# Sums of reciprocals on one core: where VectorE's sums write what nobody reads, in which row order, and how many products VectorE makes

## The chip, the cores and the metric

The kernel runs on one core of a Trainium2 chip. A core has TensorE (PE), VectorE (DVE), ScalarE (ACT), GpSimd (POOL) and SyncE (SP), each with its own instruction stream; they meet through semaphores. Sixteen DMA engines move data between the chip's main memory (HBM) and the on-chip memories. The metric is the device time of one execution in microseconds (us), lower is better.

## The reference

```python
def reference(x: np.ndarray) -> np.ndarray:
    return np.sum(1.0 / x, axis=-1).astype(np.float32)
```

`x` is 32 x 512 x 1024 float32, the absolute value of normal random numbers plus 1e-6. The result has 32 x 512 sums, each over 1024 reciprocals. That is 67.1 MB to read and 64 KB to write.

## The kernel before

The 16,384 rows are spread over 128 partitions, 128 rows on each. "Row" below means one such row index, that is, 128 rows of 1024 numbers at once, one on each partition (512 KB).

The kernel uses 1/a + 1/b = (a + b) / (a b). A row is cut into two halves of 512 numbers, a and b. For each row somebody makes the product a b, ScalarE takes its reciprocal as exp(-ln(S a b)) with S = 2^17, and VectorE multiplies this with something and adds everything up to one number per partition (the sum instruction of line 92, with the scale S and an accumulated output, followed by a tiny instruction that writes the accumulator into column c of the tile `sums`). That sum instruction also has an ordinary output, of as many elements as it has inputs, that nobody reads afterwards.

The work is cut into chunks of m = 2 rows, each a triple (m, e, v):

- A = (2, 0, 0): e = 0. GpSimd makes the products of both rows (line 136). ScalarE writes the reciprocals into a PSUM tile `rc` (line 151). VectorE sums each row whole: 1024 numbers of the row, times the reciprocal, which is read twice.
- B = (2, 2, 0): e = 2. GpSimd makes both products. TensorE adds a + b into PSUM tiles `s` by multiplying with the identity matrix (line 82, two matmuls for a row in the program, four in the profile). ScalarE writes the reciprocals back into the product tile `pr` (line 157). VectorE sums 512 numbers, `pr` times `s`.
- C = (2, 2, 1): like B, but with v = 1 the first row's product is VectorE's (line 125), from the row's first half and a copy of the second half that TensorE put into a PSUM tile `b`; GpSimd makes the product of the other row only.

`LOADS` lists the DMAs, all issued by SyncE in order: ten loads of four chunks (8 rows, 4 MB, rows 0 to 79), eight of two chunks (2 MB), eight of one (1 MB). They go into `ring`, 40 rows long, so a load waits until every reader and writer of the rows 40 earlier has finished. Of a load's chunks, the VectorE products come first in program order; then, chunk by chunk, GpSimd's products, TensorE's adds, the sums of the chunk before (`waiting`), and this chunk's ScalarE work. `keep` fixes each engine's order to the program's. So VectorE's sums always run one chunk behind.

Waits come from the tiles: whoever writes over data waits for those who read it or wrote it before, engine by engine. An instruction carries one wait; further ones become separate wait instructions in front of it. The sums of an A chunk write their useless output over the ring row they read (`out=row`); those of B and C write it over the product row they read. The product tiles `pr` come from one pool of six tiles, 4 KB on each partition; the tiles `s` from three PSUM buffers, `rc` from two, `b` from one. The last four loads are one chunk each: A, B, A, C.

Of the kernel before, what the change touches and what calls it, by code (L numbers as in the profile page):

```python
# [1 line left out]

# [6 lines left out]


@with_exitstack
def kernel(
    ctx: ExitStack,
    tc: tile.TileContext,
    x: bass.AP,
    out: bass.AP,
):

    nc = tc.nc
    f32 = mybir.dt.float32
    P = 128  # L30
    D = 1024
    H = D // 2
    F = 128

    R = 40

    S = float(2**17)

    A, B, C = (2, 0, 0), (2, 2, 0), (2, 2, 1)
    LOADS = [[A, B, A, C]] * 10 + [[A, B], [A, C]] * 4 + [[A], [B], [A], [C]] * 2

    Ln = mybir.ActivationFunctionType.Ln
    Exp = mybir.ActivationFunctionType.Exp
    mult = mybir.AluOpType.mult
    plus = mybir.AluOpType.add

    x_v = x.flatten_outer_dims().rearrange("(p f) d -> p f d", p=P)
    out_v = out.flatten().rearrange("(p f) -> p f", p=P)  # L50

    act_sets = list(get_activation_tables(nc.m.arch).keys())
    nc.scalar.add_instruction(  # L53
        mybir.InstLoadActFuncSet(
            name=nc.get_next_instruction_name(),
            act_func_set_id=act_sets.index("natural_log_exp_and_others"),
            ins=[],
            outs=[],
        )
    )  # L60

    ppool = ctx.enter_context(tc.tile_pool(name="ppool", bufs=6))
    opool = ctx.enter_context(tc.tile_pool(name="opool", bufs=1))
    spool = ctx.enter_context(
        tc.tile_pool(name="spool", bufs=3, space=bass.MemoryType.PSUM)
    )
    bpool = ctx.enter_context(
        tc.tile_pool(name="bpool", bufs=1, space=bass.MemoryType.PSUM)
    )
    rpool = ctx.enter_context(  # L70
        tc.tile_pool(name="rpool", bufs=2, space=bass.MemoryType.PSUM)
    )

    ring = opool.tile([P, R, D], f32)
    sums = opool.tile([P, F], f32)
    ident = opool.tile([P, P], f32)
    make_identity(nc, ident)
    keep = tc.keep_in_program_order

    def add(bank, *halves):  # L80
        for k, half in enumerate(halves):
            i = nc.tensor.matmul(  # L82
                bank,
                lhsT=ident,
                rhs=half,
                start=k == 0,
                stop=k == len(halves) - 1,
            )
            keep(i)

    def sum_row(c, row, fac):
        i = nc.vector.tensor_tensor_reduce(  # L92
            out=row,
            in0=row,
            in1=fac,
            scale=S,
            scalar=0.0,
            op0=mult,
            op1=plus,
            accum_out=sums[:, c : c + 1],  # L100
        )
        keep(i)

    def sum_rows(c, xc, pr, sm, rc):
        m, e = xc.shape[1], len(sm)
        for j in range(e, m):
            row = xc[:, j, :].rearrange("p (h e) -> p h e", h=2)
            sum_row(c + j, row, rc[:, j - e, :].unsqueeze(1).to_broadcast([P, 2, H]))
        for j in range(e):
            sum_row(c + j, pr[:, j, :], sm[j])  # L110

    waiting = None
    c0 = 0
    for chunks in LOADS:
        n = sum(m for m, _, _ in chunks)
        xt = ring[:, c0 % R : c0 % R + n, :]
        keep(nc.sync.dma_start(out=xt, in_=x_v[:, c0 : c0 + n, :]))

        made, q = [], 0
        for m, e, v in chunks:  # L120
            pr = ppool.tile([P, m, H], f32, tag="pr")
            for j in range(v):
                b = bpool.tile([P, H], f32, tag="b")
                add(b, xt[:, q + j, H:])
                i = nc.vector.tensor_tensor(  # L125
                    out=pr[:, j, :], in0=xt[:, q + j, :H], in1=b, op=mult
                )
                keep(i)
            made.append(pr)
            q += m  # L130

        q = 0
        for (m, e, v), pr in zip(chunks, made):
            xc = xt[:, q : q + m, :]
            if v < m:
                i = nc.gpsimd.tensor_tensor(  # L136
                    out=pr[:, v:, :], in0=xc[:, v:, :H], in1=xc[:, v:, H:], op=mult
                )
                keep(i)
            sm = []  # L140
            for j in range(e):
                s = spool.tile([P, H], f32, tag="s")
                add(s, xc[:, j, :H], xc[:, j, H:])
                sm.append(s)
            if waiting:
                sum_rows(*waiting)
            keep(nc.scalar.activation(out=pr, in_=pr, func=Ln, scale=S))  # L147
            rc = None
            if e < m:
                rc = rpool.tile([P, m - e, H], f32, tag="rc")  # L150
                i = nc.scalar.activation(  # L151
                    out=rc, in_=pr[:, e:, :], func=Exp, scale=-1.0
                )
                keep(i)
            if e:
                r = pr[:, :e, :]
                keep(nc.scalar.activation(out=r, in_=r, func=Exp, scale=-1.0))  # L157
            waiting = c0 + q, xc, pr, sm, rc
            q += m
        c0 += n  # L160
    assert c0 == F, c0
    sum_rows(*waiting)

    nc.sync.dma_start(out=out_v, in_=sums)


# [1 line left out]
_INS = ['x']  # L168
_OUTS = [((32, 512), 'float32')]


# [23 lines left out]
```

## Time and profile before

| | |
|---|---|
| median of 7 runs | 172.31 us (172.21 to 172.39) |
| the profiled execution's own time | 172.31 us |
| its span, from the first instruction to the last | 170.5 us |
| PE busy | 135.2 us, 79% |
| DVE busy | 124.6 us, 73% |
| ACT busy | 133.5 us, 78% |
| POOL busy | 133.0 us, 78% |
| granted TensorE clock | 0.998 |
| HBM read | 67.11 MB, 394 GB/s over the span |

Busy time counts arithmetic instructions, not waits, branches or the issuing of DMAs; busy PE includes pipelined matmuls whose ends are modelled. L92 is line 92 of the kernel. A row of a timeline gives start, duration, engine, line, operation, output <- input, shape, and in brackets the idle time before it with what ended it. The chain that ended last is followed back from the last instruction: at each step to what released it, or to the instruction before it on its engine. A stretch's row gives, for each engine, the busy time and the number of instructions, then the granted clock, the mean busy share of the sixteen DMA engines and their rate in GB/s.

### The profile page before, as it was taken

The numbers are of one execution on the slowest core, as the hardware profiler recorded it, in microseconds if no ns is written. First come the engines' busy times: TensorE is split into PE (matmuls) and PEld (weight loads), VectorE is DVE, ScalarE is ACT, GpSimd is POOL, SyncE is SP. The second block draws the span as 40 slices with busy tenths as digits, with TensorE's granted clock in tenths as the row PEclk, the third lists the DMA queues.
The fourth block names the chain that finished last, engine by engine and source line by source line (L and its number), as shares of the span: only waits on it lengthen the run. The fifth ranks groups of instructions, "written<-read, shape, count | busy, mean of one in ns | idle before, by whom it ended". The sixth has DMA issues, their size and how long they took to land.

```text
span 170.5 us, 1320 instructions
## 1 busy us (share of the span) xinstructions
PE 135.2 (79%) x288; PEld 51.9 (30%) x288; DVE 124.6 (73%) x272; ACT 133.5 (78%) x129; POOL 133.0 (78%) x70
## 2 busy tenths in 40 slices
PE   0008999888889888796988887979999998896790
PEld 0003333332332333242333322333334332342240
DVE  0001777777987777787777769889998988889683
ACT  3002979979787997959799797899999988999790
POOL 1008969696996969589696969999999799996930
PEclk9999999999999999999999999999999999999999
DMA  5999999999999999999999999999999999999300
GB/s 208 415 454 407 454 423 446 415 461 415 448 407 446 415 454 419 438 425 430 430 438 423 438 396 427 427 427 430 427 427 423 427 413 423 421 421 417 148 0 15
DMA packets 3895, 67.25 MB, mean 394 GB/s; under 512 B 432, under 2 KB 560, under 8 KB 560
## 3 DMA queue, kind: packets, MB, share of 16 engines
q1 hardware_dynamic: 3888, 67.18, 92.4%
q8 instruction: 2, 0.03, 0.1%
q14 instruction: 5, 0.04, 0.1%
HBM read 67.11 MB, written 0.07 MB: 394 GB/s over the span
## 4 chain that ended last, share of the span: by engine, by line
DMA 66%; POOL 22%; issue 6%; DVE 3%; ACT 1%; DVEq 0%; POOLq 0%
DMA ring<-in_x_dram 66%; POOL pr L136 22%; DVE ring L92 2%; ACT pr L147 1%; ACT rc L151 1%; DVE pr L92 0%; DVE pr L125 0%; DVEq L190 0%; POOLq L136 0%; DVE sums L92 0%; DVEq L92 0%
## 5 line engine op out<-in xcount | busy, mean ns | idle before, releaser
L136 POOL TENSOR_TENSOR pr<-ring 128x1024 f32<-128x1024 f32 x64 | 132.3, 2097 | 29.9 <-DMA ring<-in_x_dram 29.6
L82 PE MATMUL s<-ring,ident 128*128 128x512 f32 x256 | 120.1, 605 | 15.5 <-DVE sums L92 13.9
L92 DVE CUSTOM_DVE_ANT_1 ring<-ring,rc 128x1024 f32<-128x1024 f32 x64 | 75.6, 1219 | 26.9 <-ACT rc L151 22.8
L147 ACT ACTIVATE pr<-pr 128x1024 f32<-128x1024 f32 x64 | 67.3, 1051 | 30.0 <-POOL pr L136 29.6
L82 PEld LDWEIGHTS s<-ring,ident 128*128 128x128 f32 x256 | 46.6, 191 | 87.1 <-issue 47.9
L92 DVE CUSTOM_DVE_ANT_0 pr<-pr,s 128x512 f32<-128x512 f32 x64 | 41.3, 682 | 0.7 <-ACT pr L157 0.7
L157 ACT ACTIVATE pr<-pr 128x1024 f32<-128x1024 f32 x32 | 33.8, 1058 | 1.0
L151 ACT ACTIVATE rc<-pr 128x1024 f32<-128x1024 f32 x32 | 32.9, 1028 | 1.0
L82 PE MATMUL b<-ring,ident 128*128 128x512 f32 x32 | 18.6, 665 | 15.9 <-DMA ring<-in_x_dram 15.7
L125 DVE TENSOR_TENSOR pr<-ring,b 128x512 f32<-128x512 f32 x16 | 10.9, 683 | 15.7 <-PE b L82 15.6
L82 PEld LDWEIGHTS b<-ring,ident 128*128 128x128 f32 x32 | 5.2, 196 | 26.9 <-issue 15.0
L92 DVE DVE_READ_ACCUMULATOR2_ANT sums<- 128x1 f32 x128 | 10.6, 83 | 0.0
L53 ACT ACT_TABLE_LOAD x1 | 1.3, 1283 | 0.7 <-PEq L179 0.7
masks.py:197 POOL MEMSET ident<- 128x128 f32 x1 | 0.2, 204 | 0.3 <-POOLq L179 0.3
masks.py:199 POOL TENSOR_SCALAR_AFFINE_SELECT ident<-ident 128x128 f32<-128x128 f32 x1 | 0.3, 292 | 0.1
L179 POOL MEMSET const-float32-0.0<- 128x1 f32 x1 | 0.1, 98 | 0.2 <-issue 0.2
L179 POOL MEMSET const-uint8-127<- 128x1 uint8 x1 | 0.1, 103 | 0.0
L179 POOL MEMSET const-bfloat16-1.0<- 128x1 bf16 x1 | 0.1, 101 | 0.0
L179 POOL MEMSET const-float32-1.0<- 128x1 f32 x1 | 0.1, 98 | 0.0
## 6 DMA issues: line engine op xcount, KB each, us to landing
ring<-in_x_dram SPq DMA_DIRECT2D x10, 4096.0 KB, 37.6
ring<-in_x_dram SPq DMA_DIRECT2D x8, 2048.0 KB, 36.9
ring<-in_x_dram SPq DMA_DIRECT2D x8, 1024.0 KB, 28.4
out_dram<-sums SPq DMA_DIRECT2D x1, 64.0 KB, 1.5
```

The source lines that it names most:

```text
L53: nc.scalar.add_instruction(mybir.InstLoadActFuncSet(name=nc.get_next_instruction_name(), act_func_set_id=act_sets.index("natural_log_exp_ ...
L82: i = nc.tensor.matmul(bank, lhsT=ident, rhs=half, start=k == 0, stop=k == len(halves) - 1,)
L92: i = nc.vector.tensor_tensor_reduce(out=row, in0=row, in1=fac, scale=S, scalar=0.0, op0=mult, op1=plus, accum_out=sums[:, c : c + 1],)
L125: i = nc.vector.tensor_tensor(out=pr[:, j, :], in0=xt[:, q + j, :H], in1=b, op=mult)
L136: i = nc.gpsimd.tensor_tensor(out=pr[:, v:, :], in0=xc[:, v:, :H], in1=xc[:, v:, H:], op=mult)
L147: keep(nc.scalar.activation(out=pr, in_=pr, func=Ln, scale=S))
L151: i = nc.scalar.activation(out=rc, in_=pr[:, e:, :], func=Exp, scale=-1.0)
L157: keep(nc.scalar.activation(out=r, in_=r, func=Exp, scale=-1.0))
L179: nc = _bacc.Bacc("TRN2", target_bir_lowering=False, num_devices=1)
```

## The change

Four edits. In the first 80 rows, the loads alternate between A, B, A, B and A, B, A, C, so VectorE makes one product in 16 rows there, not one in 8 (five fewer in all; GpSimd makes those five). The sum of the first row of an A chunk writes its unread output over the chunk's own product tile, which ScalarE has read by then, and not over the ring; the second row's still goes over its ring row. The sums of a B or C chunk go through their rows in reverse. The product tiles come from two sets of four, one for A chunks (`pr`) and one for B and C chunks (`ps`), instead of one set of six.

```diff
-    LOADS = [[A, B, A, C]] * 10 + [[A, B], [A, C]] * 4 + [[A], [B], [A], [C]] * 2
+    LOADS = [[A, B, A, B], [A, B, A, C]] * 5 + [[A, B], [A, C]] * 4 + [[A], [B], [A], [C]] * 2
...
-    ppool = ctx.enter_context(tc.tile_pool(name="ppool", bufs=6))
+    ppool = ctx.enter_context(tc.tile_pool(name="ppool", bufs=4))
...
-    def sum_row(c, row, fac):
+    def sum_row(c, row, fac, out=None):
         i = nc.vector.tensor_tensor_reduce(
-            out=row,
+            out=row if out is None else out,
             in0=row,
...
         for j in range(e, m):
             row = xc[:, j, :].rearrange("p (h e) -> p h e", h=2)
-            sum_row(c + j, row, rc[:, j - e, :].unsqueeze(1).to_broadcast([P, 2, H]))
-        for j in range(e):
+            sum_row(
+                c + j,
+                row,
+                rc[:, j - e, :].unsqueeze(1).to_broadcast([P, 2, H]),
+                pr[:, e : e + 2, :] if j == e and m - e > 1 else None,
+            )
+        for j in reversed(range(e)):
             sum_row(c + j, pr[:, j, :], sm[j])
...
-            pr = ppool.tile([P, m, H], f32, tag="pr")
+            pr = ppool.tile([P, m, H], f32, tag="ps" if e else "pr")
```

## The prediction

> **What bounds the kernel now.** I read the page's slices first, then its chain, then the chain's last 40 us in order of time.
>
> ```profile
> DMA  5999999999999999999999999999999999999300
> DMA packets 3895, 67.25 MB, mean 394 GB/s; under 512 B 432, under 2 KB 560, under 8 KB 560
> q8 instruction: 2, 0.03, 0.1%
> q14 instruction: 5, 0.04, 0.1%
> DMA 66%; POOL 22%; issue 6%; DVE 3%; ACT 1%; DVEq 0%; POOLq 0%
> ```
>
> The DMA row is 9 from slice 2 to slice 36: the input stream never pauses. No arithmetic engine is that full. The two "instruction" rows are small packets in which the chip loads program code; they come back below.
>
> The stream's pace is read from POOL, which takes each 4 MB load as it lands (timeline, POOL):
>
> ```profile
> 62.40 8.28 POOL L136 TENSOR_TENSOR pr<-ring 128x1024 f32<-128x1024 f32 x4 [1.46 <-DMA ring<-in_x_dram]
> 72.96 8.25 POOL L136 TENSOR_TENSOR pr<-ring 128x1024 f32<-128x1024 f32 x4 [2.29 <-DMA ring<-in_x_dram]
> 82.68 8.25 POOL L136 TENSOR_TENSOR pr<-ring 128x1024 f32<-128x1024 f32 x4 [1.47 <-DMA ring<-in_x_dram]
> 92.39 8.27 POOL L136 TENSOR_TENSOR pr<-ring 128x1024 f32<-128x1024 f32 x4 [1.46 <-DMA ring<-in_x_dram]
> ```
>
> A load comes every 9.72 us, POOL needs 8.27 and idles 1.46. One interval is 10.56: something delayed a load by 0.84 us. Loads are issued 37.6 us (median of the page's DMA issues) before they land, so four are queued at once, and a ring slot could come free some 27 us later (37.6 less one load) before the stream noticed.
>
> The tail, by the chain in order of time and DVE's timeline:
>
> ```profile
> 131.49 25.59 DMA ring<-in_x_dram
> 157.24 2.36 POOL pr L136
> 159.71 2.38 POOL pr L136
> 162.11 1.07 ACT pr L147
> 163.20 1.04 ACT rc L151
> 164.23 0.03 DVEq L92
> 164.35 0.60 DVE ring L92
> ```
>
> ```profile
> 161.81 0.69 DVE L92 CUSTOM_DVE_ANT_0 pr<-pr,s 128x512 f32<-128x512 f32 x1 [0.66 <-ACT pr L157]
> ...
> 166.64 0.68 DVE L92 CUSTOM_DVE_ANT_0 pr<-pr,s 128x512 f32<-128x512 f32 x1
> ```
>
> So the end is the landing at 157.08 of the last B load plus two POOL products, ACT, and four sums on DVE. Who makes that landing late? Each load ends with sixteen small writes, one per DMA engine (the 432 packets under 512 B are 27 transfers times 16). Their times in the trace's packets show thirteen engines finishing the last load by 159.62 us and three late ones, at 160.49, 160.72 and 161.56. The stretches of the stream's end show the same:
>
> ```profile
> 159.60:160.40 0.80, 0.80 (x3) 0.21 (x2) 0.80 (x3) 0.77 (x1) 0.69 (x1) 1.00 0.17 72
> 160.50:160.70 0.20, 0.20 (x1) 0.00 (x0) 0.20 (x1) 0.19 (x1) 0.20 (x1) 1.00 0.10 41
> 160.75:161.50 0.75, 0.13 (x1) 0.00 (x0) 0.39 (x2) 0.75 (x1) 0.75 (x1) 1.00 0.05 22
> ```
>
> The last two columns are DMA share and GB/s; one engine of sixteen is 0.0625. Three engines, then two, then a single one are still at work.
>
> Why are those three late? Following each engine's end from load to load (9.70 us apart), single engines step back for good, each right behind a code packet: 8 KB at 46.25 us steps one by 0.97 us; 16 KB at 64.73 another by 1.56; 8 KB at 105.5 to 105.9 two, one of them the engine of 46.25 again, by 0.97; 16 KB at 131.37 a fifth by 1.54; 8 KB at 154.08 the engine of 46.25 a third time, by about 0.96. That last step is why the landings of the end, 2.48 apart till 153.75, jump to 157.08. Its engine had 0.14 us less delay than the slowest until then; it ends 0.84 later than the next (161.56 against 160.72). A load counts as landed 0.45 us after the slowest engine's write.
>
> Whose code? By the trace's records (waits counted), DVE had started 69, 199 to 201 and 325 instructions at 46.25, 105.5 to 105.9 and 154.08: steps of about 128, on the same DMA engine each time. ACT stands at 67 at the 8 KB of 73.04 and POOL at 68 at that of 105.5. PE stands at 195 and 449 at the two 16 KB packets, 254 apart. So a queue fetches when it has passed about 64, 192 and 320 instructions (PE: 192, 448, next 704).
>
> **The change part by part.** The profiled execution took 172.31 us for a span of 170.5; the median is 172.31, so its sums stand for the median.
>
> *Five fewer products on VectorE.* Gone: 5 DVE products of 0.683, 10 identity matmuls of 0.665 with their weight loads. Five POOL products grow from 1.279 to 2.370 us, 5.5 us in all, one per second 4 MB load. POOL's starts lie 2.33 apart, so such a load takes 3 x 2.33 + 2.37 = 9.36 us against 9.72 between landings: it still fits, with 0.36 idle. If that cover went, the next load has 1.46 idle, and the ring's 27 us lie behind. From row 80 the loads are unchanged, and POOL waits for landings again at 136.5, 141.5, 153.9 and 157.2. Cost: nothing.
>
> *First sum of an A chunk writes the product tile.* 32 of the 64 1.219 us sums keep their size. No row shows this sum with another destination; from below and above the nearest rows are the sums that write that tile over 512 elements (0.682) and the ring write (1.219); I take 1.219, same elements and reads. All but the last lie beside the stream. The wait for POOL moves to the second sum, which starts 1.15 later, long after it is met. In the tail, the first sum started 0.12 us behind ACT's end (164.23 to 164.35, over a separate wait); the B sum at 161.81, whose ACT wait is in the sum itself, 0.03 behind. Gain 0.09 in that hand-over.
>
> *Two pools of 4 instead of one of 6.* POOL's products for A now wait for DVE's sum of eight chunks earlier, about 19 us, where DVE trails by some 7 (product at 92.39, sums over at 99.35). Nothing waits: nothing.
>
> *Reverse rows.* The last chunk C sums row 1 first, so it needs the second of PE's sums first. That semaphore rose at 166.63, 4.62 us behind the last landing (162.01); the first's at 164.91. Now DVE started C at 166.64, so the old order hid it and the new one cannot. Elsewhere PE is some 3 us ahead of DVE: nothing.
>
> *Instructions.* Built, the programs hold on DVE 364 before and 322 after (5 products and 37 separate waits fewer), POOL 123 and 132, ACT 178 and 173, SP 73 and 74. PE loses about 14 of 589 records. DVE's last sum is then behind instruction 316, so its third fetch, due near 320, falls behind the input stream or never. The others keep their number: POOL's and ACT's second would be due near 192, PE's third near 704, and SP passes 64 only in the closing.
>
> *The sum.* Without that step the slowest engine ends at 160.72 instead of 161.56: landings -0.84 from the last B load on; the last one at 161.17. POOL follows (it was free at 156.25, the B load lands at 156.23). DVE would be free for C at 166.64 - 0.84 - 0.09 = 165.71, but PE's second sum comes at 161.17 + 4.62 = 165.79, and 0.12 for the hand-over gives 165.91. Before it was 166.64: -0.73. Two sums, the store and the closing follow as before. 172.31 - 0.73 = **171.58 us**.
>
> Bounds: the hand-over between 0.03 and 0.12 (I take 0.12, the row with a separate wait, as C will have); the step between 0.84 and 1.07, if the engine ending at 160.72 is relieved too (its PE fetch moves by some 16 instructions). That gives 171.26 to 171.58.
>
> A rule that speaks against this: the Trainium skill, "Runtime: NRT & Kernel Launch", section "Instruction fetch mechanics", has code streamed in 16 KiB blocks by the sequencer's own DMA queue, the cost mostly hidden. Hidden it is from DVE here, which works through 154.08 without a gap (153.71 to 154.37, then the next); the DMA engine's delay of 0.96 us is in the trace all the same, and DVE's packets are 8 KB. By the rule the sum would have no -0.84 and would be 172.42.
>
> **The rivals.**
>
> *The stream ends as before.* For it: the link from code packet to engine is by timing and counts, and the packet could be another queue's or come at another count. Then only the reversed tail counts: C at 166.63 + 0.12 = 166.75, +0.11: 172.42.
>
> *Slower: a code packet hits the engine that serves DVE.* PE's two came on two engines, DVE's on one, so the choice isn't explained. If PE's second went to DVE's, that would end at 160.60 + 1.54 = 162.14, landing at 162.59, 0.58 later than now: C at 167.21 + 0.12 against 166.64, 173.0. It decides as soon as any engine ends behind 161.56. Against it: DVE's engine was the same three times.
>
> *POOL as the bound.* It would need more than 9.72 / 4 = 2.43 us per product, and then over two loads 19.4 us against 9.36 + 8.27; the products measure 2.37 throughout. That loses almost nothing even so.
>
> *More gained.* If PE's packets left the late engines too, the stream would end with the thirteen (159.62). Then POOL would be the limit: free at 153.32 from the product before, it would start the tail's next one at 153.4 instead of 153.88 and the last B's 1.4 earlier; DVE would reach C at 166.64 - 1.44 - 0.09 = 165.1: 170.8.
>
> **How the numbers follow.** Forecast 0.78, stream as before 0.11, slower 0.07 (POOL in it), more gained 0.04. A difference under 0.2% (0.34 us) is about what this kernel's times cannot tell from none. The forecast and "more" are faster: 0.82; the second is within 0.2%: 0.11; slower 0.07. The range runs from 171.2, the lower bound of the forecast, to 172.45, the stream as before.
>
> **What would show it.** Right: one code packet less before the stream's end, none near 154; landings 2.48 apart to the last, at about 161.2; C's first sum waiting on PE. Product loads of about 9.36 on POOL with 0.36 idle. Wrong: a jump of 0.8 in the landings behind row 120, or a fourth late engine.

## The result and the profile after

The changed kernel takes 171.77 us (median of 13 runs, 171.59 to 171.95) against 172.34 us of the kernel before on the same chips (31 runs). The ratio is 0.9967, 95% interval 0.996 to 0.9975: 0.57 us, or 0.33%, faster. The forecast was 171.58, with a range of 171.2 to 172.45; the measured time is in that range, and 0.19 above the sum and its own bounds (171.26 to 171.58). The profiled execution took 171.90 us for a span of 170.1, so it lies 0.13 above the median.

The page after, in the lines that answer to those of before (span, the DMA row of the slices, code packets, chain):

```profile
span 170.1 us, 1267 instructions
DMA  6999999999999999999999999999999999999400
q8 instruction: 2, 0.03, 0.1%
q14 instruction: 5, 0.03, 0.0%
DMA 80%; POOL 7%; issue 3%; PE 3%; ACT 3%; DVE 2%; SPq 1%; POOLq 0%; DVEq 0%
```

The stream is as full as before. What the code rows say is small but it is the point: queue 14 moved 0.03 MB, not 0.04 (its count stays at 5, because a packet of 24 bytes at 0.16 us is counted in it). One 8 KB packet of VectorE's has left the span: by the packets' times it now comes at 170.76, behind the last instruction of the span. In the end of the stream, 150 to 161 us, no code packet is left at all (DMA view of that stretch, all its queues):

```profile
## 3 DMA queue, kind: packets, MB, share of 16 engines
q1 hardware_dynamic: 537, 3.85, 84.1%
```

Before, the same view had a row "q14 instruction: 1" for the packet of 154.08. POOL and TensorE show what came of it (timelines after; the last row is TensorE's first work on the last load):

```profile
73.11 9.31 POOL L141 TENSOR_TENSOR pr<-ring 128x1024 f32<-128x1024 f32 x4 [2.42 <-DMA ring<-in_x_dram]
82.83 8.28 POOL L141 TENSOR_TENSOR pr<-ring 128x1024 f32<-128x1024 f32 x4 [0.41 <-DMA ring<-in_x_dram]
92.54 9.35 POOL L141 TENSOR_TENSOR pr<-ring 128x1024 f32<-128x1024 f32 x4 [1.43 <-DMA ring<-in_x_dram]
153.96 8.73 POOL L141 TENSOR_TENSOR pr<-ring 128x1024 f32<-128x1024 f32 x4 [0.58 <-DMA ring<-in_x_dram]
```

```profile
161.30 1.13 PE L82 MATMUL b<-ring,ident 128*128 128x512 f32 x2 [1.17 <-DMA ring<-in_x_dram]
```

The loads with four whole products take POOL 9.31 to 9.35 us and leave 0.41 before the next one: the fit that was worked out. From 153.96 on POOL works without a break; before, it had to wait at 157.24 for a late landing. The last load lands at 161.25 instead of 162.01.

The stretches of the stream's end after, in the same columns as before, lose the single engine that was still at work till 161.56:

```profile
159.60:160.60 1.00, 0.52 (x2) 0.00 (x0) 1.00 (x3) 0.97 (x2) 1.00 (x1) 1.00 0.18 74
160.90:161.25 0.35, 0.00 (x0) 0.00 (x0) 0.30 (x3) 0.13 (x1) 0.35 (x1) 1.00 0.00 0
```

Three engines (0.18 is three of sixteen) end almost together now, at 160.65, 160.70 and 160.83 by their small writes; the other thirteen are through by 159.53. The chain of the tail has a new last link (chain in order of time, then one row of the waits):

```profile
141.49 19.76 DMA ring<-in_x_dram
161.30 1.13 PE b L82 x2
162.42 3.45 PE s L82 x8
165.90 0.05 DVEq L92
166.04 0.69 DVE pr L92
```

```profile
DVE pr L92 <- PE s L82: 0.2, 1, 0.2
```

Before, the chain ran over POOL and ACT to VectorE. Now it runs from the last landing straight over TensorE, and the last chunk's first sum is the only one in the kernel that waits for TensorE's sums, for 0.17 us.

### The profile page after: what moved, and what is told of

Its sections match the earlier page's. It is cut to its first block, busy times and chain, and to the rows that moved or that the text cites. A ratio compares the mean times of both kernels' runs of the same rounds, so it can differ in the third digit from the quotient of the medians.

```text
span 170.1 us, 1267 instructions
## 1 busy us (share of the span) xinstructions
PE 133.3 (78%) x278; PEld 51.3 (30%) x278; DVE 122.4 (72%) x267; ACT 133.9 (79%) x129; POOL 138.3 (81%) x70
## 4 chain that ended last, share of the span: by engine, by line
DMA 80%; POOL 7%; issue 3%; PE 3%; ACT 3%; DVE 2%; SPq 1%; POOLq 0%; DVEq 0%
DMA ring<-in_x_dram 80%; POOL pr L141 7%; PE s L82 2%; ACT pr L152 2%; DVE ring L92 1%; DVE pr L92 1%; SPq L122 1%; PE b L82 1%; ACT rc L156 1%; ACT pr L162 0%; DVE sums L92 0%; POOLq L141 0%; DVEq L92 0%; DVEq L195 0%
## 5 line engine op out<-in xcount | busy, mean ns | idle before, releaser
L141 POOL TENSOR_TENSOR pr<-ring 128x1024 f32<-128x1024 f32 x64 | 137.6, 2181 | 23.8 <-DMA ring<-in_x_dram 22.4
L82 PE MATMUL s<-ring,ident 128*128 128x512 f32 x256 | 124.0, 624 | 31.1 <-DMA ring<-in_x_dram 15.5
L82 PEld LDWEIGHTS s<-ring,ident 128*128 128x128 f32 x256 | 47.4, 195 | 104.4 <-issue 63.6
L92 DVE CUSTOM_DVE_ANT_1 pr<-ring,rc 128x1024 f32<-128x1024 f32 x32 | 39.1, 1221 | 43.9 <-ACT rc L156 43.9
L92 DVE CUSTOM_DVE_ANT_1 ring<-ring,rc 128x1024 f32<-128x1024 f32 x32 | 38.9, 1216 | 0.0
L82 PE MATMUL b<-ring,ident 128*128 128x512 f32 x22 | 12.0, 629 | 1.4 <-DMA ring<-in_x_dram 1.4
L130 DVE TENSOR_TENSOR pr<-ring,b 128x512 f32<-128x512 f32 x11 | 7.5, 684 | 0.8 <-PE b L82 0.7
L82 PEld LDWEIGHTS b<-ring,ident 128*128 128x128 f32 x22 | 4.0, 202 | 9.3 <-DMA ring<-in_x_dram 7.1
```

Source lines behind the costliest of these rows:

```text
L82: i = nc.tensor.matmul(bank, lhsT=ident, rhs=half, start=k == 0, stop=k == len(halves) - 1,)
L92: i = nc.vector.tensor_tensor_reduce(out=row if out is None else out, in0=row, in1=fac, scale=S, scalar=0.0, op0=mult, op1=plus, accum_out ...
L130: i = nc.vector.tensor_tensor(out=pr[:, j, :], in0=xt[:, q + j, :H], in1=b, op=mult)
L141: i = nc.gpsimd.tensor_tensor(out=pr[:, v:, :], in0=xc[:, v:, :H], in1=xc[:, v:, H:], op=mult)
```

## The experiments

The theory: the gain is one code packet of VectorE's that no longer comes while the input streams. Its rivals: VectorE's lighter work, the moved waits or the row order brought the gain. All kernels were timed beside the kernel before on the same chip; the chips differ in noise, so each time is to be held against its own "before".

### One part alone: the reversed rows

```diff
-        for j in range(e):
+        for j in reversed(range(e)):
             sum_row(c + j, pr[:, j, :], sm[j])
```

> The kernel before with one edit: the sums of a B or C chunk go through their rows in reverse. Its VectorE program holds 357 instructions (before 364). Theory (the gain is a code packet that no longer comes while the input streams): VectorE still passes instruction 320 some 33 instructions before its end, so the third packet comes at about 156 us, the slowest DMA engine still ends near 161.56, and the reversed tail adds what it added after the change, a hand-over of 0.12 to 0.17 us behind TensorE's second sum: 172.4 to 172.5. Rival (the row order itself brought the gain): 171.8.

Measured: 172.84 us, before 172.52; ratio 1.0021, 0.9995 to 1.0046. No gain, so the rival is out; the loss is larger than expected but not clear of none. POOL's timeline shows the packet delaying the load after the one that it delayed in the kernel before, where it came at 154.08 and POOL waited at 157.24 (here it came at 156.11, with 324 VectorE instructions started):

```profile
159.85 3.76 POOL L136 TENSOR_TENSOR pr<-ring 128x1024 f32<-128x1024 f32 x2 [1.04 <-DMA ring<-in_x_dram]
```

The engine ends at 161.72, the last landing is at 162.18, and the last chunk's first sum starts at 166.96 instead of 166.64, 0.32 later. The span is 0.46 longer (170.97 against 170.51); the other 0.14 lies behind the store and is taken up below.

### One part alone: the redirected sums and the two sets of tiles

The diff is that of the changed kernel without its new `LOADS` and without `reversed`.

> The kernel before with the first sum of an A chunk written over the product tile and with the two sets of four product tiles; row order and loads as before. Its VectorE program holds 339 instructions. Theory: instruction 320 is passed about 15 before the end, at 163 us or later, behind the input stream, so the third packet costs nothing; the last load lands near 161.2, TensorE's order isn't reversed, so VectorE is the one that ends last: about 171.5, a little under the changed kernel. Rival (the gain needs all parts together, or comes from fewer VectorE products): 172.3.

Measured: 172.10, before 172.52, ratio 0.9965 (0.9939 to 0.999) on a noisy chip; its profiled execution took 171.23. It was run again below. There is a gain here without a single product less. The tail's chain comes over POOL, ScalarE and VectorE, not over TensorE; its last pieces are:

```profile
163.29 0.94 DVE pr L92
164.23 0.20 issue
164.44 0.08 DVE sums L92
164.52 1.13 DVE ring L92
165.65 0.01 DVE sums L92
165.66 0.30 DVE pr L92
```

The first sum of the last A chunk follows ScalarE's end (163.26) by 0.03, where it was 0.12 before: the separate wait is gone, as worked out. One thing was off: the packet came at 160.59, with 315 instructions started, not at 163, and fell into the last load, which landed at 161.30. It was still too late to delay the last B load, and POOL no longer waited for that one.

### One part alone: fewer products

```diff
-    LOADS = [[A, B, A, C]] * 10 + [[A, B], [A, C]] * 4 + [[A], [B], [A], [C]] * 2
+    LOADS = [[A, B, A, B], [A, B, A, C]] * 5 + [[A, B], [A, C]] * 4 + [[A], [B], [A], [C]] * 2
```

> The kernel before with the new list of loads alone: VectorE makes every sixteenth product in the first 80 rows. Its VectorE program holds 357 instructions. Theory: the third packet still comes before the stream ends, near 156 us: 172.3, no change. Rival (less VectorE work brought the gain): 171.8. Rival (POOL becomes the bound): above 172.7.

Measured: 172.38, before 172.52; ratio 0.999, 0.9967 to 1.0013. No change that can be told from none; but the interval reaches from 0.57 us less to 0.22 us more, so the time alone doesn't rule the rival out. The trace shows the packet inside the stream, at 158.96 (not near 156), a last landing at 162.24 and the same span as before, 170.5. That less work on VectorE is not the gain is decided by the kernel above, which gains with every product in place, and by the one with 40 memsets below.

### Putting the instructions back without the work

A tile of 128x1 that nobody reads is set to zero by VectorE, n times behind each of the loads 2 to 9 of the changed kernel:

```diff
+    scratch = opool.tile([P, 1], f32)
+
+    def filler(n):
+        for _ in range(n):
+            keep(nc.vector.memset(scratch, 0.0))
...
         c0 += n
+        if 8 < c0 <= 72:
+            filler(1)    # 8 in all; filler(5): 40; filler(20): 160
```

> The changed kernel with 8 tiny VectorE memsets of a 128x1 tile that nobody reads, one behind each of the loads 2 to 9. Its VectorE program holds 330 instructions (the changed kernel 322, before 364). Theory (VectorE's third code packet comes when it passes about instruction 320): that is now 10 instructions before the end, behind the input stream: 171.8, as the changed kernel. Rival (the gain is VectorE work that was taken away): the same 171.8, since 8 x 0.06 us is nothing.

> The changed kernel with 40 such memsets, five behind each of the loads 2 to 9. Its VectorE program holds 362 instructions. Theory: the third code packet is back inside the stream, at 154 to 156 us, on the DMA engine that already had two; the last landing returns from 161.25 to about 162.0 and the last chunk's sum, which waits for TensorE, to 166.8: 172.5, all of the gain gone, though every sum, wait and product is the changed kernel's. Rival (the gain is work or waits taken away): 40 memsets of some 0.06 us lie in VectorE's idle time in the first 80 rows: 171.8.

> The changed kernel with 160 such memsets, twenty behind each of the loads 2 to 9. Its VectorE program holds 482 instructions. Theory: VectorE passes 320 and 448 inside the stream, two more packets of about 0.97 us each on the same DMA engine, which ends at 160.65 + 1.94 = 162.6 instead of the changed kernel's last 160.83: 1.75 us more: 173.5. Rival (the memsets' own work): 20 x 0.06 = 1.2 us per load beside 9.7 us: 171.8.

Measured, before 172.30 in all three: with 8 memsets 171.78 (ratio 0.9968, 0.9956 to 0.998); with 40, 172.64 (1.0022, 1.0012 to 1.0031); with 160, 173.83 (1.0115, 1.0084 to 1.0146). Forty memsets of 59 ns, 2.4 us in all and spread over 70 us in which VectorE has idle time, cost 0.86 us more than eight of them, which is more than the whole gain. Eight cost nothing: VectorE's third packet comes at 163.69 there, behind the stream, the stretch from 150 to 161 us has no queue but the input's, and the last chunk starts at 165.92 (166.04 and 165.88 in two profiles of the changed kernel):

```profile
q1 hardware_dynamic: 532, 3.81, 83.2%
```

```profile
165.92 0.69 DVE pr L92
```

The profile of the kernel with 40 has the packet back in the stretch from 150 to 161 us (queue 14; by its time 154.69, with 326 VectorE instructions started), and its last landing and last chunk (TensorE's timeline, then the chain's last sums) are those of the kernel before with the reversed tail:

```profile
q14 instruction: 1, 0.01, 0.2%
```

```profile
162.04 1.12 PE L82 MATMUL b<-ring,ident 128*128 128x512 f32 x2 [1.16 <-DMA ring<-in_x_dram]
```

```profile
166.62 0.03 issue
166.64 0.05 DVEq L92
166.69 0.09 issue
166.78 0.69 DVE pr L92
```

The time with 160 is a median of six runs, of which two took 175.3 us. With 160 memsets there are two more packets, at 105.91 and 157.47 (322 and 449 instructions started). The stretch that was empty in the changed kernel has one engine at work, nearly to its end, and the last landing is at 163.22:

```profile
160.80:162.70 1.90, 0.33 (x1) 0.00 (x0) 1.86 (x7) 1.19 (x2) 1.81 (x1) 1.00 0.06 26
```

This engine ends at 162.76: two packets cost some 2.1 us over the changed kernel's 160.65, or 1.05 each, where 0.97 was expected. So the time follows the number of VectorE packets inside the stream: two, three and four packets go with 171.78, 172.64 and 173.83 us, though the added instructions do nothing that is used.

### Another engine's packet

In the changed kernel, the same filler with ScalarE's activation in place of the memset, five behind each of the loads 2 to 9:

```diff
+    def filler(n):
+        for _ in range(n):
+            keep(nc.scalar.activation(out=scratch, in_=scratch, func=Exp, scale=-1.0))
```

> The changed kernel with 40 tiny ScalarE activations of a 128x1 tile that nobody reads, five behind each of the loads 2 to 9, and one memset for the tile. Its ScalarE program holds 213 instructions (the changed kernel 173). Theory: ScalarE passes instruction 192 inside the stream and draws a second packet, on a DMA engine that isn't among the three late ones (it would go from at most 159.5 to about 160.5, against 160.83): a code packet costs only where its DMA engine ends last: 171.8. Rival (any code packet inside the stream costs its delay): 172.6. Second rival (the activations crowd ScalarE, 5 x 0.2 us of its 1.3 us idle per load): above 172.

Measured: 172.02, before 172.30; ratio 0.9986, 0.9977 to 0.9995. It draws the additional packet (148.46, 188 ScalarE instructions started). A fourth engine is late, but not the last: it ends at 160.00, the three at 160.39, 160.48 and 160.56.

```profile
159.75:159.95 0.20, 0.15 (x1) 0.00 (x0) 0.20 (x1) 0.20 (x1) 0.20 (x1) 1.00 0.30 123
160.10:160.35 0.25, 0.00 (x0) 0.00 (x0) 0.25 (x1) 0.25 (x1) 0.25 (x1) 1.00 0.15 66
```

The last landing, 161.01, isn't later than the 161.25 of the changed kernel, and the last chunk's first sum starts at 165.79 (166.04 there). So this packet costs nothing at the end of the stream, where a packet on the engine that ends last cost 0.9 us. The time itself, 172.02, isn't the 171.8 that was expected, and the second rival had forecast more than 172; but the last chunk doesn't start later, so the activations don't hold up the tail. That the run is 0.24 above the one with 8 memsets lies behind the store.

### Without the reversed tail

```diff
     def sum_rows(c, xc, pr, sm, rc):
+        last = c + xc.shape[1] == F
...
-        for j in reversed(range(e)):
+        for j in range(e) if last else reversed(range(e)):
```

> The changed kernel, but the last chunk alone sums its rows in the old order. Its VectorE program holds 323 instructions, so no third packet before the stream ends. Theory: the last landing stays near 161.25; the last chunk's first sum no longer waits for TensorE's second sum, and starts when VectorE is free, 165.8 instead of 166.04: 0.2 us less than the changed kernel, 171.55. Rival (TensorE doesn't hold the end): 171.77 as the changed kernel.

Measured: 171.99, before 172.52; ratio 0.9963, 0.994 to 0.9986. Against its own before that is 0.53 less, where 0.75 was expected (171.55 against 172.3); on this noisy chip the interval reaches from 0.24 to 1.04 less, so the times don't tell the two apart. The profile shows the mechanism: the chain's sum of the last chunk is at 165.91 and no longer behind TensorE.

```profile
164.76 1.13 DVE ring L92
165.90 0.01 DVE sums L92
165.91 0.05 DVE pr L92
```

Its store is issued at 167.15, 0.22 earlier than in the changed kernel; but the span is only 0.10 shorter (170.01 against 170.11). Half of the time is lost again between the store and the end.

### The versions without reversal, beside the changed kernel

Three kernels on one chip: the changed kernel with `for j in range(e)` throughout; the redirected sums with two sets of tiles alone, again; and the changed kernel itself.

> The changed kernel with the rows of B and C chunks summed in the old order throughout. Its VectorE program holds 333 instructions, SyncE's 73 (changed kernel 322 and 74). Theory: instruction 320 is passed near 163 us, behind the stream; the last landing stays near 161.2; TensorE's second sum is hidden again (0.2 to 0.25 us less), and the closing behind the store is as short as before, 2.54 instead of 2.74 us from the store's issue: 171.3. Rival (the reversed order is part of the gain): 171.8 or more.

> The kernel of e2_redirect again, beside the changed kernel on the same chip. Its 320th VectorE instruction falls at about 160.6 us, into the last load: 171.3 to 171.5, up to 0.2 above e9_forward when the packet still delays the last landing.

> The changed kernel itself, for comparison with the two others on the same chip: 171.77, and 0.4 to 0.5 above e9_forward.

Measured, before 172.28: 171.57 (ratio 0.9953, 0.9941 to 0.9966; runs from 171.16 to 171.70), 171.34 (0.9945, 0.9932 to 0.9957; 171.20 to 171.48) and 171.72 (0.9968, 0.9955 to 0.998; 171.72 to 171.80). So the redirected sums and two sets of tiles alone have the lowest median of the kernels tried, and the whole gain: each of this kernel's five runs lies below each of the changed kernel's six, by 0.38 us in the median. Its packet came at 160.60 again and held the last landing at 161.30, against 161.09 in the changed kernel here. That landing isn't on its chain, which comes over POOL and ScalarE, and POOL makes the last three whole products without waiting for the late B load of the kernel before:

```profile
153.76 7.33 POOL L141 TENSOR_TENSOR pr<-ring 128x1024 f32<-128x1024 f32 x3 [0.58 <-DMA ring<-in_x_dram]
```

The version with the new loads missed its 171.3, and the changed kernel is 0.15 above it, not 0.4 to 0.5. Its profiled execution's last landing was at 161.52 instead of 161.2, with no packet to account for it; the DMA engine that ended first was late as well, by 0.15 against the profile after, so its whole stream ran later. Why is open.

## Why the prediction was right

**The step of the landings** was right. -0.84 was expected for all landings from the last B load on; the last one moved by 0.76 in the profile after (162.01 to 161.25), and by 0.92 in the changed kernel's second profile (161.09). The three late engines were named with 160.60 (VectorE's), 160.49 and 160.72 (TensorE's); they ended at 160.65 to 160.83. The experiments with memsets show the cause itself, not only the timing.

**The count** was right: VectorE's third packet left the stream because 364 instructions became 322. Over all runs VectorE's third packet starts when 315 to 329 of its instructions have started. Which of the parts brought the count down could be read from the built programs, and the single parts bear it out: the reversal (357) and the new loads (357) leave the packet inside the stream, at 156.11 and 158.96, and show no gain; the redirection (339) moves it to 160.6, too late for the last B load, and that is enough.

**The reversed rows** were right in mechanism and somewhat too small: TensorE's second sum rose at 165.87 (165.79 expected) and the hand-over took 0.17 instead of 0.12. The last chunk starts at 166.04, so -0.60, not -0.73. In the second profile of the changed kernel it starts at 165.88, so -0.76. The first sum of an A chunk, taken at 1.219 us without a row for it, measured 1.221.

**What failed** is the sentence "Two sums, the store and the closing follow as before". The two sums do; the closing does not. From the store's issue to the end of the span it took 2.54 us before and 2.75 after (the store's rows before and after):

```profile
167.97 0.34 SPq L164 DMA_DIRECT2D out_dram<-sums  x1
167.37 0.34 SPq L169 DMA_DIRECT2D out_dram<-sums  x1
```

So -0.60 became about -0.40 in the first profile (171.90 against 172.31), and -0.76 became -0.54 in the second. The closing is the 0.2 us by which the time missed the sum. That the time is in the range says less: the range's upper end was the rival in which the stream ends as before.

By the trace's records the kernels whose SyncE program has 73 instructions, and whose VectorE passes 320 well before the end, need 2.54 (before, the two single parts without reversal, the changed kernel without reversal). The reversed kernels with 74 need 2.67 or 2.68. SyncE's waits stand one after the other, some 0.06 apart. Before, three separate waits follow the one for the store's landing; in the kernels with 74 there is one wait more, and the wait for the landing is the first and not the second, so five follow it. Two waits more behind the landing are the 0.13. I had both counts and took the extra one for nothing. The changed kernel (VectorE 322) needs 2.75 and 2.76, the two kernels with VectorE at 323 need 2.98 (SyncE 74) and 2.86 (SyncE 73): 0.31 and 0.32 above their kind. In the one with activations VectorE's DRAIN record in the closing comes 0.48 us behind its wait, against 0.11 in the one with 8 memsets, and the third packet follows at 170.43. So it seems that VectorE itself stands still for some 0.3 us where it asks for code; that this is the request and not something else beside it was not tried. It would account for the 0.24 of the kernel with activations, and for the time that the one with the old order in the last chunk loses behind its store.

**The rest** held: five products more on POOL cost nothing. The tiles' new waits cost nothing that shows: the profile puts one POOL wait of 1.0 us, up to 136.53, down to a VectorE sum, but in both kernels the load had landed at 136.40 and POOL started at 136.53. Of the rivals, "slower" asked for an engine ending behind 161.56; the kernel with 160 memsets, whose last engine ends at 162.76, is that case, by packets of VectorE's and not of TensorE's.

The Trainium skill, "Runtime: NRT & Kernel Launch", section "Instruction fetch mechanics", calls the cost of crossing a block of code mostly hidden. For VectorE that agrees with the trace before, where it worked through 154.08 without a gap; for the DMA engine that carried the packet it does not, since that one lost 0.96 us.

## What to carry to other kernels

In a kernel bound by its input stream, look for who is last among the sixteen DMA engines at the stream's end, and what delayed that one. Here program code came over the same engines, and the number of an engine's instructions, separate waits included, decided how many code packets fell into the stream. So removing 37 waits, which the tail gained next to nothing from directly (0.09 us in one hand-over), moved a packet that cost 0.8 us, and adding 40 idle instructions cost 0.9 us. Behind the stream the tail has its own chain: an order that was free all along (which row first) counts there, and so does each wait behind the last store.

## What the runs showed of the hardware that was not expected

- A code packet costs its DMA engine more than its own duration: inside the stream, packets of 0.31 to 0.42 us (8 KB) stepped their engine back by 0.7 us (ScalarE's, in the kernel with activations) to 1.05 us, and those of 16 KB, before, of 1.06 and 1.10 us, by 1.56 and 1.54. Why a step is longer than its packet is open.
- By the steps of the engines' ends (a packet's record doesn't name its engine), VectorE's packets all came over one DMA engine, whose delays add up: 160 memsets made it end 2.1 us later than in the changed kernel.
- VectorE seems to stop for some 0.3 us where it asks for code. In the closing 0.31 us showed when its program had 323 instructions and not 330, and some 0.08 when it had 322; at 154.08, inside the program of the kernel before, no gap shows. No run isolates it.
